# First stage of an encoder kernel: weights' products, x's transposes and the value groups in one written order

## The chip, the cores and the metric

The kernel runs on one core of a Trainium2 chip. The metric is the device time of one execution in microseconds, the median of several runs. The engines are TensorE (PE in the profile, its weight loads PEld), VectorE (DVE), ScalarE (ACT), GpSimd (POOL) and SyncE (SP, which here only issues DMAs).

## The reference

Two layers, each a token mixer and a convolutional MLP, on x of shape (1, 256, 1024) in float32. Only the beginning of the first layer matters here:

```python
def _rmsnorm(x, g):
    y = xf * lax.rsqrt(jnp.mean(xf * xf, axis=-1, keepdims=True) + EPS)
    return (y * g)

xn = _rmsnorm(h, norm1[layer])
u, q, k, v, g_pool, g_attn = jnp.split(xn @ w_in, SPLITS, axis=-1)
...   # pooling mixer on u, dilated attention on q, k, v, gates, output projection
h = h + ...
h = h + _conv_ffn(_rmsnorm(h, norm2[layer]), ...)
```

The values `v` are 1536 columns of `w_in`: three groups of 512.

## The kernel before

Every float32 product is made of three products of split numbers: a high part (`xuh`, `wh`) and a rest (`xul`, `wl`), with `hh`, `lh` and `hl` for high times high, rest of x times high weights, high x times rest of weights. ScalarE casts the high part, VectorE subtracts to get the rest. x's 256 tokens are two halves `t` of 128, its 1024 channels eight chunks `k` of 128.

The first layer starts with the values, since a row's norm can be applied to the finished sums. `begin_values_of_x` records, in an order written out by hand (`manual_schedule`), the first group of values: x comes in parts by SyncE's and ScalarE's DMA queues, TensorE transposes it (`turn_x`, `xt_ps`), ScalarE and VectorE split it (`keep`), and they split the weights chunk by chunk, scaled by the norm's gains (`split(k)`, `both(k)`: high part L255, rest L256; the gains are turned in `begin` and kept in `gcol`). `square` sums the squares of x's rows, GpSimd makes the root (`rs`), and `whole` adds `xuh` and `xul` into `xu` again, half of the channels at a time. The tiles of the weights in this group are named m (chunks 0 to 3), ybig (4, 5) and at (6, 7); from the second group on `wh` and `wl`, in pieces of two chunks.

`first_values` holds the second and the third group of values (L930), and scales `xu` by the root (`rows`, `r_ps`) and the gains into `x2`, which the products of queries, keys and pooling read (`by_tokens`, `t_ps`, L691). Before the change a scheduler places these instructions, and those of `load_params`, by its own costs. A group's four pieces are held until both halves of the tokens are done, one half after the other:

```python
for t in range(2):
    for n, (_, (wh, wl)) in enumerate(held):
        for j in range(2):
            ...
```

Weights come through a ring of three raw buffers of 1 MB (`W.load`, SyncE) and a ring of five split pieces. `W.get` splits some pieces ahead of use. A load waits until the raw buffer before it in the ring has been split. What follows the values (L1250 on) is written in its own order and is the same before and after.

Of the kernel before, what the change touches and what calls it, by code (L numbers as in the profile page):

```python
# [280 lines left out]
def encoder(ctx, tc, x, w_in, w_pool, pool_scale, w_a, w_b, w_o, norm1, norm2, w_up, conv_w,  # L281
# [85 lines left out]
    def begin():  # L367


        rows8 = sm.tile([KD, P], F32, tag="gain", bufs=1, name="grows")  # L370
        first, second = W.load_by(4), W.load_by(2)

        def part_of_x(queue, t, cc):
            queue.dma_start(out=h[:, t, cc], in_=xv[:, t, cc])

        nc.scalar.dma_start(out=rows8, in_=norm1[0].rearrange("(k p) -> k p", p=P))
        for t, queue in enumerate((nc.sync, nc.scalar)):
            part_of_x(queue, t, slice(0, 256))
# [12 lines left out]
        nc.vector.memset(mhalf, -0.5)  # L391
        ps = mmp.tile([P, P], F32, tag="mm", name="gain_ps")
        warm(ps, ones, WARM[0])
        nc.tensor.transpose(ps[:, 0:KD], rows8, ident[:KD, :KD])
        nc.vector.tensor_copy(gcol, ps[:, 0:KD])
        ps = mmp.tile([P, P], F32, tag="mm", name="warm_ps")
        warm(ps, ones, WARM[1])
        return lambda widths: warm(ps, ones, widths)
# [10 lines left out]
    def load_params():  # L409

        nc.sync.dma_start(out=edge.rearrange("p a b -> p (a b)"), in_=edges[0].partition_broadcast(P))
        for l in range(DEPTH):
# [3 lines left out]
            nc.sync.dma_start(out=rowst[88:96, :], in_=pool_scale[l].rearrange("(f p) -> f p", p=P))  # L416
            pt = mmp.tile([P, 512], F32, tag="mm", name="prm_ps")
            nc.tensor.transpose(pt[:, :96], rowst, ident[:96, :96])
            nc.vector.tensor_copy(prm[:, l, :], pt[:, :96])
            nc.vector.tensor_scalar_mul(hps[:, l, :], prm[:, l, 88:96], 0.5)  # L420

    bt = const.tile([P, HPG, NT * P], F32, name="bt")

# [343 lines left out]
    def begin_values_of_x():  # L767


        more = begin()  # L770
        W.gains = gcol

        raw_x = [
# [26 lines left out]
        def square(t, n):  # L800
            cc = HALVES[n]
            junk = sm.tile([P, 512], F32, tag="p", bufs=3, name="junk")
            if n == 0:
                nc.scalar.activation(
                    junk, h[:, t, cc], AF.Square, scale=D**-0.5, accum_out=ss[t][:, n : n + 1]
                )
            else:
                nc.vector.scalar_tensor_tensor(
                    out=junk, in0=h[:, t, cc], scalar=1.0 / D, in1=h[:, t, cc],
                    op0=ALU.mult, op1=ALU.mult, accum_out=ss[t][:, n : n + 1],  # L810
                )
            if n == 0:
                nc.gpsimd.tensor_scalar_add(ss[t][:, 3:4], ss[t][:, 0:1], EPS)
            else:
                nc.gpsimd.tensor_add(out=ss[t][:, 3:4], in0=ss[t][:, 3:4], in1=ss[t][:, 1:2])
                return nc.gpsimd.tensor_tensor(out=rs[t], in0=ss[t][:, 3:4], in1=mhalf, op=ALU.pow)

        def whole(n, tag):

            ks = slice(4 * n, 4 * n + 4)  # L820
            f = big.tile([P, 4, 2, P], F32, tag=tag, name="xu")
            nc.vector.tensor_add(out=f, in0=xuh[:, ks].bitcast(F32), in1=xul[:, ks].bitcast(F32))
            return f

        ps = [v_tile() for _ in range(2)]
# [27 lines left out]
        every = ("hh", "lh", "hl")  # L853
        keep = [turn_x((t,), 0, 2) for t in range(2)]
        more(WARM[2])
# [9 lines left out]
        products((0, 0, ("hl",)), (1, 0, ("hl",)))  # L865
        both(2)
        products((0, 1, ("hh", "lh")), (1, 1, ("hh", "lh")), (0, 1, ("hl",)), (1, 1, ("hl",)))
        both(3)
        square(0, 0)
        square(1, 0)  # L870
        square(0, 1)
        pool = square(1, 1)
        products((0, 2, ("hh", "lh")), (1, 2, ("hh", "lh")))
        keep = turn_x((0,), 4, 4)
        products((0, 2, ("hl",)), (1, 2, ("hl",)))
        keep()
        products((0, 3, every))
        keep = turn_x((1,), 4, 4)
        both(4)
        keep()  # L880
        W.load(5)
        products((1, 3, every), (0, 4, every))
        both(5)
        products((1, 4, every), (0, 5, every))
        f0 = whole(0, "q0")
        both(6)
        products((1, 5, every), (0, 6, every))
        both(7)
        products((1, 6, every), (0, 7, every))
        f1 = whole(1, "k0")  # L890
        pe = products((1, KD - 1, ("hh", "hl", "lh")))
# [6 lines left out]
        return rs, raw_x, (f0, f1), ps, pe  # L898

    def first_values(rs, raw_x, fs, done, pe, keep_values):  # L900
# [5 lines left out]
        with tc.issue_after(pe.ins):  # L906
            for t in range(2):
                nc.tensor.transpose(rows[:, t, :], rs[t][:, 0:1].to_broadcast([P, P]), ident)
        for k in range(0, KD, 2):
            f = fs[k // 4][:, k % 4 : k % 4 + 2]  # L910
            for j in range(2):
                nc.vector.scalar_tensor_tensor(
                    out=f[:, j], in0=f[:, j], scalar=gcol[:, k + j : k + j + 1], in1=rows,
                    op0=ALU.mult, op1=ALU.mult,
                )
            oh, ol = (x2[:, k : k + 2, part] for part in (0, 1))
            nc.scalar.copy(out=oh, in_=f)
            nc.vector.tensor_sub(out=ol, in0=f, in1=oh.bitcast(F32))
        ps = done
        for g in range(NG):  # L920
            held = [W.get() for _ in range(4)] if g + 1 < NG else []
            for t in range(2):
                keep_values(t, g, ps[t], rs)
            ps = [v_tile() for _ in range(2)]
            for t in range(2):
                for n, (_, (wh, wl)) in enumerate(held):
                    for j in range(2):
                        k = 2 * n + j
                        for m, (a, w) in enumerate(((xuh, wh), (xuh, wl), (xul, wh))):
                            nc.tensor.matmul(  # L930
                                ps[t], a[:, k, t, :], w[:, j, :], start=(k + m == 0),
                                stop=(k == KD - 1 and m == 2),
                            )
            for i, _ in held:
                W.free(i)
        return x2

    for l in range(DEPTH):
# [21 lines left out]
        if l == 0:  # L960
            with tc.manual_schedule():
                begun = begin_values_of_x()
            x2 = first_values(*begun, keep_values)
        else:
            for g in range(NG):
                held = begun[0] if g == 0 else [W.get() for _ in range(4)]
# [9 lines left out]
                    W.free(i)  # L976

        if l == 0:
            load_params()
# [515 lines left out]
```

## Time and profile before

| | |
|---|---|
| median of three runs | 855.9 us (854.67 to 855.96) |
| profiled execution | 854.77 us; span of its instructions 853.0 us |
| busy in the span | TensorE 844.8, its weight loads 705.7, VectorE 620.6, ScalarE 490.5, GpSimd 33.6 us |
| granted clock of TensorE | 0.998 |
| values, from the first product to the first t_ps | 5.73 to 41.15 us |

The page's busy times are for the whole program; the stage of the change is the first 5% of it. A row of the timeline has the start, the duration, engine, line, operation, output and inputs, shapes, how many such instructions follow one another, and in brackets the idle time before them with what ended it. TensorE's rows overlap, since its matmuls are pipelined: the distance from start to start is what one costs.

### The profile page before, as it was taken

What the parts mean: (1) busy time and instruction counts of PE and PEld (TensorE: products, weight loads), DVE (VectorE), ACT (ScalarE), POOL (GpSimd) and SP (SyncE); (2) the same over time, 40 slices, a digit from 0 to 9 for tenths busy, and PEclk for the clock granted to TensorE, in tenths of its full rate; (3) what the DMA queues carried; (4) which work ended last, traced back from release to release, by engine and by line L of the source; (5) the groups of instructions that cost most, each with busy time, mean ns of one, the idle gap of its engine ahead of it and who ended that gap; (6) DMA issues with size and microseconds to landing.
All of it is one profiled execution on the core that took longest, in us unless ns stands there. A gap on an engine that the chain in (4) does not pass through costs nothing.

```text
span 853.0 us, 11006 instructions
## 1 busy us (share of the span) xinstructions
PE 844.8 (99%) x3925; PEld 705.7 (83%) x3925; DVE 620.6 (73%) x885; ACT 490.5 (58%) x723; POOL 33.6 (4%) x96
## 2 busy tenths in 40 slices
PE   9999999999999999999999999999999999999997
PEld 7888888888888888888888888888888888888885
DVE  7958777757765976878655687868567767777774
ACT  7744566654543865657545454577454556556663
POOL 1700000000010000000000000000000100000000
PEclk9999999999999999999999999999999999999999
DMA  9699997895657879986726899868777489799941
GB/s 326 212 302 285 294 292 233 252 293 210 222 209 263 300 250 301 293 284 233 245 100 216 261 280 330 245 226 264 242 257 269 147 289 315 230 288 288 296 145 50
DMA packets 147678, 214.03 MB, mean 251 GB/s; under 512 B 7768, under 2 KB 68640, under 8 KB 147624
## 3 DMA queue, kind: packets, MB, share of 16 engines
q1 hardware_dynamic: 147320, 212.93, 76.8%
q8 instruction: 31, 0.51, 0.2%
q10 hardware_dynamic: 304, 0.40, 0.1%
q14 instruction: 23, 0.19, 0.1%
HBM read 186.02 MB, written 27.28 MB: 250 GB/s over the span
## 4 chain that ended last, share of the span: by engine, by line
PE 98%; DMA 1%; SPq 0%; DVE 0%; ACT 0%; issue 0%; DVEq 0%; ACTq 0%
PE t_ps L691 64%; PE v_ps L691 6%; PE res_ps L610 6%; PE res_ps L608 6%; PE res_ps L609 6%; PE v_ps L930 3%; PE pool_ps L595 1%; PE v_ps L839 1%; PE o_ps L1200 1%; PE s_ps L1152 1%; PE s_ps L1147 1%; PE o_ps L1196 1%; PE xt_ps L522 1%; DMA h<-in_x_dram 1%; PE xt_ps L787 0%; SPq L184 0%
## 5 line engine op out<-in xcount | busy, mean ns | idle before, releaser
L245 DVE TENSOR_TENSOR wl<-raw,wh 128x1024 fp32r<-128x1024 f32 x274 | 332.0, 1221 | 159.0 <-ACT wh L243 158.1
L691 PE MATMUL t_ps<-wh,x 128*128 128x512 f32 x1408 | 438.8, 390 | 0.0
L243 ACT CAST wh<-raw 128x1024 fp32r<-128x1024 f32 x274 | 286.3, 1052 | 211.5 <-PE t_ps L691 146.4
L691 PEld LDWEIGHTS t_ps<-wh,x 128*128 128x128 f32 x1408 | 264.3, 188 | 54.8
L691 PE MATMUL t_ps<-wl,x 128*128 128x512 f32 x704 | 273.9, 389 | 0.0
L691 PEld LDWEIGHTS t_ps<-wl,x 128*128 128x128 f32 x704 | 132.2, 188 | 27.3
L610 PE MATMUL res_ps<-wh,actk 128*128 128x512 f32 (+1 forms) x184 | 70.0, 380 | 0.0
L609 PE MATMUL res_ps<-wl,actq 128*128 128x512 f32 (+1 forms) x184 | 69.9, 380 | 0.0
L608 PE MATMUL res_ps<-wh,actq 128*128 128x512 f32 (+1 forms) x184 | 69.8, 380 | 0.0
L691 PE MATMUL t_ps<-wh,po 128*128 128x512 f32 x128 | 41.4, 395 | 0.0
L608 PEld LDWEIGHTS res_ps<-wh,actq 128*128 128x128 f32 x184 | 34.6, 188 | 6.6
L609 PEld LDWEIGHTS res_ps<-wl,actq 128*128 128x128 f32 x184 | 34.6, 188 | 6.6
L610 PEld LDWEIGHTS res_ps<-wh,actk 128*128 128x128 f32 x184 | 34.6, 188 | 6.6
L487 POOL TENSOR_SCALAR ss<-ss 128x1 f32<-128x1 f32 x8 | 2.2, 279 | 773.5 <-ACT junk L480 773.5
L691 PEld LDWEIGHTS t_ps<-wh,po 128*128 128x128 f32 x128 | 24.0, 188 | 4.9
L1373 ACT ACTIVATE y<-a,prm 128x256 f32<-128x256 f32 x44 | 26.5, 602 | 1.5
L608 PE MATMUL res_ps<-wh,m 128*128 128x512 f32 (+1 forms) x72 | 26.5, 368 | 0.0
L609 PE MATMUL res_ps<-wl,m 128*128 128x512 f32 (+1 forms) x72 | 26.3, 365 | 0.0
L741 DVE STREAM_TRANSPOSE crossing<-t_ps 128x512 f32<-128x512 f32 x40 | 26.2, 693 | 0.0
L610 PE MATMUL res_ps<-wh,m 128*128 128x512 f32 (+1 forms) x72 | 26.0, 366 | 0.0
L691 PE MATMUL v_ps<-wh,x 128*128 128x512 f32 x80 | 25.6, 392 | 0.0
L691 PE MATMUL t_ps<-wl,po 128*128 128x512 f32 x64 | 24.9, 390 | 0.0
(193 smaller groups left out, 931.1 us busy)
## 6 DMA issues: line engine op xcount, KB each, us to landing
raw<-in_w_in_dram SPq DMA_DIRECT2D x58, 1024.0 KB, 6.8
raw<-in_w_up_dram SPq DMA_DIRECT2D x40, 1024.0 KB, 7.1
raw<-in_w_down_dram SPq DMA_DIRECT2D x22, 1024.0 KB, 6.0
crossing<-crossing SPq DMA_DIRECT2D x22, 512.0 KB, 8.5
crossing<-way SPq DMA_DIRECT2D x16, 512.0 KB, 4.8
raw<-in_w_a_dram SPq DMA_DIRECT2D x8, 1024.0 KB, 5.1
raw<-in_w_o_dram SPq DMA_DIRECT2D x8, 1024.0 KB, 7.0
zga<-crossing SPq DMA_DIRECT2D x40, 128.0 KB, 3.7
```

The costliest lines, as they stand in the source:

```text
L243: inst = nc.scalar.copy(out=h, in_=src)
L245: inst = self.rests[i] = nc.vector.tensor_sub(out=l, in0=src, in1=h.bitcast(F32))
L522: nc.tensor.transpose(pt[:, k, :], xn[:, c0 : c0 + P], ident)
L595: nc.tensor.matmul(out, w(k), x, start=(steps is first and k == 0), stop=(steps is last and k == nk - 1), skip_group_check=turns["rest"],)
L608: nc.tensor.matmul(ps, ah, wh, start=first, stop=False, skip_group_check=on)
L609: nc.tensor.matmul(ps, ah, wl, start=False, stop=False, skip_group_check=on)
L610: nc.tensor.matmul(ps, al, wh, start=False, stop=last, skip_group_check=on)
L691: nc.tensor.matmul(ps, x2[:, 2 * n + j, part, t, :], w[:, j, :], start=(n + m == 0), stop=(n == last and m == 5),)
L741: nc.vector.transpose(out=y[:, t].rearrange("p q c j -> p c q j"), in_=rows[t])
L839: return nc.tensor.matmul(ps[t], a[:, k, t, :], w[:, k % 2, :], start=first, stop=last)
L930: nc.tensor.matmul(ps[t], a[:, k, t, :], w[:, j, :], start=(k + m == 0), stop=(k == KD - 1 and m == 2),)
L1373: nc.scalar.activation(y, a, AF.Identity, bias=b, scale=w1)
```

## The change

- `begin`: half of x's first part goes ahead of the gains on ScalarE's queue; seven warming matmuls and one more of full width in place of six and two of half width; the gains are turned between the two transposes of x.
- `begin_values_of_x`: another order, below. Both halves of the squares go to ScalarE. `whole` goes to GpSimd, both calls after the squares. The high part of chunk 2 goes to VectorE.
- `load_params` issues its DMAs behind the fifth weight load, and its transposes come one after each value group.
- `first_values`: written order. Each piece serves both halves of the tokens and is then freed; the scaling of `xu` is spread between the pieces.

```diff
-WARM = ((P,) * 6, (P // 2,), (P // 2,))
+WARM = ((P,) * 7, (P,))
-        nc.scalar.dma_start(out=rows8, in_=norm1[0].rearrange("(k p) -> k p", p=P))
         for t, queue in enumerate((nc.sync, nc.scalar)):
             part_of_x(queue, t, slice(0, 256))
+        nc.scalar.dma_start(out=rows8, in_=norm1[0].rearrange("(k p) -> k p", p=P))
...
-            nc.vector.tensor_add(out=f, in0=xuh[:, ks].bitcast(F32), in1=xul[:, ks].bitcast(F32))
+            nc.gpsimd.tensor_add(out=f, in0=xuh[:, ks].bitcast(F32), in1=xul[:, ks].bitcast(F32))
...
+        def one_by_one(*steps):
+            products(*((t, k, (kind,)) for k, kind in steps for t in range(2)))
...
-        products((0, 0, ("hh",)), (1, 0, ("hh",)), (0, 0, ("lh",)), (1, 0, ("lh",)))
+        one_by_one((0, "hh"), (0, "lh"))
+        both(1)
+        one_by_one((1, "hh"), (1, "lh"))
         keep = turn_x((0, 1), 2, 2)
-        both(1)
+        _, lo, hi = split(2)
+        hi()
         keep()
...
+        one_by_one((0, "hl"), (1, "hl"))
         both(3)
+        one_by_one((2, "hh"), (3, "hh"), (2, "lh"))
+        keep = [turn_x((0,), 4, 4)]
+        one_by_one((3, "lh"))
+        keep.append(turn_x((1,), 4, 4))
+        both(4)
+        W.load(5)
+        turn_params = load_params()
+        for k in keep:
+            k()
+        one_by_one((2, "hl"), (3, "hl"))
+        both(5)
+        one_by_one((4, "hh"), (4, "lh"), (4, "hl"))
         square(0, 0)
         square(1, 0)
+        both(6)
+        one_by_one((5, "hh"), (5, "lh"), (5, "hl"))
+        both(7)
         square(0, 1)
         pool = square(1, 1)
...
+        fs = [whole(n, tag) for n, tag in enumerate(("q0", "k0"))]
+        one_by_one((6, "hh"), (6, "lh"), (6, "hl"))
+        products((0, 7, every))
+        products((1, KD - 1, ("hh", "hl", "lh")))
...
+        for g in range(NG - 1):
             ps = [v_tile() for _ in range(2)]
+            for n in range(4):
+                at = 4 * g + n
+                for begun in scales[max(0, at - 1) : at]:
+                    next(begun)
+                i, (wh, wl) = W.get()
+                for begun in scales[max(0, at - 2) : at]:
+                    next(begun)
+                for j in range(2):
+                    k = 2 * n + j
+                    for m, (a, w) in enumerate(((xuh, wh), (xuh, wl), (xul, wh))):
+                        for t in range(2):
                             nc.tensor.matmul(
...
                 W.free(i)
+                if n == 0:
+                    for t in range(2):
+                        if g == 0:
+                            nc.tensor.transpose(
+                                rows[:, t, :], rs[t][:, 0:1].to_broadcast([P, P]), ident
+                            )
+                    for t in range(2):
+                        keep_values(t, g, done[t], rs)
+            if g < DEPTH:
+                turn_params(g)
+            done = ps
```

TensorE's queue at the beginning, from the first products on (xt_ps are the transposes of x), before:

```order
L839 MATMUL v_ps<-m_138,xuh 128x512 x2
L839 MATMUL v_ps<-m_138,xul 128x512 x2
L787 MATMUL xt_ps<-ident,h 128x128 x4
L839 MATMUL v_ps<-m_138,xuh 128x512 x3
L839 MATMUL v_ps<-m_138,xul 128x512
```

and after:

```order
L841 MATMUL v_ps<-m_138,xuh 128x512 x2
L841 MATMUL v_ps<-m_138,xul 128x512 x2
L841 MATMUL v_ps<-m_138,xuh 128x512 x2
L841 MATMUL v_ps<-m_138,xul 128x512 x2
L795 MATMUL xt_ps<-ident,h 128x128 x4
L841 MATMUL v_ps<-m_138,xuh 128x512 x8
L841 MATMUL v_ps<-m_138,xul 128x512 x2
L795 MATMUL xt_ps<-ident,h 128x128 x4
```

Four products of chunk 1 now stand ahead of the second transposes, and ten products instead of twelve between those and the third.

ScalarE's queue from chunk 1 to the second group's first weights (ybig and at are the weights of chunks 4 to 7, junk the squares), before:

```order
L255 ACTIVATE m_138<-raw_92,gcol 128x512
L793 CAST xuh<-xt_ps 128x512
L255 ACTIVATE m_138<-raw_92,gcol 128x512 x2
L804 ACTIVATE junk,ss<-h 128x512 x2
L793 CAST xuh<-xt_ps 128x4x128
L255 ACTIVATE ybig_205<-raw_100,gcol 128x512
L793 CAST xuh<-xt_ps 128x4x128
L255 ACTIVATE ybig_205<-raw_100,gcol 128x512
L255 ACTIVATE at_228<-raw_100,gcol 128x512 x2
L255 ACTIVATE wh_252<-raw_103,gcol 128x512 x2
```

and after:

```order
L255 ACTIVATE m_138<-raw_92,gcol 128x512
L801 CAST xuh<-xt_ps 128x512
L255 ACTIVATE m_138<-raw_92,gcol 128x512
L255 ACTIVATE ybig_188<-raw_100,gcol 128x512
L801 CAST xuh<-xt_ps 128x4x128 x2
L255 ACTIVATE ybig_188<-raw_100,gcol 128x512
L811 ACTIVATE junk,ss<-h 128x512 x2
L255 ACTIVATE at_224<-raw_100,gcol 128x512 x2
L811 ACTIVATE junk,ss<-h 128x512 x2
L255 ACTIVATE wh_261<-raw_103,gcol 128x512 x2
```

The first ybig (chunk 4) now stands ahead of both casts of x's second half, and four squares ahead of the second group's weights.

GpSimd's queue from the squares on, after (before, L440 followed the last power at once):

```order
L815 TENSOR_SCALAR ss<-ss 128x1 x2
L817 TENSOR_TENSOR ss<-ss 128x1
L818 TENSOR_TENSOR rstd<-ss,mhalf 128x1
L817 TENSOR_TENSOR ss<-ss 128x1
L818 TENSOR_TENSOR rstd<-ss,mhalf 128x1
L824 TENSOR_TENSOR xu<-xuh,xul 128x1024 x2
L448 COPY fsb<-rbt 4x1 x4
```

Both sums of x stand behind the powers and ahead of the small copies of the bias table. On VectorE, where they stood between the weights' rests, nothing takes their place.

More of the change, by code (lines that the diff above doesn't have):

```diff
@@ L391, in begin, with gains @@
         nc.vector.memset(mhalf, -0.5)
-        ps = mmp.tile([P, P], F32, tag="mm", name="gain_ps")
+        ps = mmp.tile([P, P], F32, tag="mm", name="warm_ps")
         warm(ps, ones, WARM[0])
[L394 to L398, printed above, removed]
+        def gains():
+            gp = mmp.tile([P, P], F32, tag="mm", name="gain_ps")
+            nc.tensor.transpose(gp[:, 0:KD], rows8, ident[:KD, :KD])
+            nc.vector.tensor_copy(gcol, gp[:, 0:KD])
+        return gains, lambda widths: warm(ps, ones, widths)
     def warm(ps, a, widths):
@@ L411, in load_params @@
         nc.sync.dma_start(out=edge.rearrange("p a b -> p (a b)"), in_=edges[0].partition_broadcast(P))
+        rows = []
         for l in range(DEPTH):
@@ L416, in load_params, with turn @@
             nc.sync.dma_start(out=rowst[88:96, :], in_=pool_scale[l].rearrange("(f p) -> f p", p=P))
+            rows.append(rowst)
+        def turn(l):
             pt = mmp.tile([P, 512], F32, tag="mm", name="prm_ps")
-            nc.tensor.transpose(pt[:, :96], rowst, ident[:96, :96])
+            nc.tensor.transpose(pt[:, :96], rows[l], ident[:96, :96])
             nc.vector.tensor_copy(prm[:, l, :], pt[:, :96])
             nc.vector.tensor_scalar_mul(hps[:, l, :], prm[:, l, 88:96], 0.5)
+        return turn
     bt = const.tile([P, HPG, NT * P], F32, name="bt")
@@ L767, in begin_values_of_x @@
     def begin_values_of_x():
-        more = begin()
+        gains, more = begin()
         W.gains = gcol
@@ L802, in square @@
             junk = sm.tile([P, 512], F32, tag="p", bufs=3, name="junk")
[L803 to L811, printed above, removed]
+            nc.scalar.activation(
+                junk, h[:, t, cc], AF.Square, scale=D**-0.5, accum_out=ss[t][:, n : n + 1]
+            )
             if n == 0:
@@ L851, in products @@
             return last
+        def one_by_one(*steps):
+            products(*((t, k, (kind,)) for k, kind in steps for t in range(2)))
         every = ("hh", "lh", "hl")
-        keep = [turn_x((t,), 0, 2) for t in range(2)]
-        more(WARM[2])
+        keep = [turn_x((0,), 0, 2)]
+        gains()
+        keep.append(turn_x((1,), 0, 2))
+        more(WARM[1])
         _, lo, hi = split(0)
@@ L860, in begin_values_of_x @@
         lo()
-        products((0, 0, ("hh",)), (1, 0, ("hh",)), (0, 0, ("lh",)), (1, 0, ("lh",)))
+        one_by_one((0, "hh"), (0, "lh"))
+        both(1)
+        one_by_one((1, "hh"), (1, "lh"))
         keep = turn_x((0, 1), 2, 2)
-        both(1)
+        _, lo, hi = split(2)
+        hi()
         keep()
-        products((0, 0, ("hl",)), (1, 0, ("hl",)))
-        both(2)
-        products((0, 1, ("hh", "lh")), (1, 1, ("hh", "lh")), (0, 1, ("hl",)), (1, 1, ("hl",)))
+        lo()
+        one_by_one((0, "hl"), (1, "hl"))
         both(3)
+        one_by_one((2, "hh"), (3, "hh"), (2, "lh"))
[10 more added lines that the diff above has]
+        one_by_one((4, "hh"), (4, "lh"), (4, "hl"))
         square(0, 0)
         square(1, 0)
+        both(6)
+        one_by_one((5, "hh"), (5, "lh"), (5, "hl"))
+        both(7)
         square(0, 1)
         pool = square(1, 1)
[L873 to L891, printed above, removed]
+        fs = [whole(n, tag) for n, tag in enumerate(("q0", "k0"))]
+        one_by_one((6, "hh"), (6, "lh"), (6, "hl"))
+        products((0, 7, every))
+        products((1, KD - 1, ("hh", "hl", "lh")))
         W.load(6)
@@ L897, in begin_values_of_x, with first_values @@
         W.queue_behind((act, dve, pool), 4)
-        return rs, raw_x, (f0, f1), ps, pe
-    def first_values(rs, raw_x, fs, done, pe, keep_values):
+        return rs, raw_x, fs, turn_params, ps
+    def first_values(rs, raw_x, fs, turn_params, done, keep_values):
         xuh, xul = raw_x
@@ L905, in first_values, with scale @@
         rows = mmp.tile([P, 2, P], F32, tag="mm", name="r_ps")
[L906 to L909, printed above, removed]
+        def scale(k):
             f = fs[k // 4][:, k % 4 : k % 4 + 2]
@@ L915, in first_values @@
                 )
+            yield
             oh, ol = (x2[:, k : k + 2, part] for part in (0, 1))
             nc.scalar.copy(out=oh, in_=f)
+            yield
             nc.vector.tensor_sub(out=ol, in0=f, in1=oh.bitcast(F32))
[L919 to L923, printed above, removed]
-            ps = [v_tile() for _ in range(2)]
[L925 to L929, printed above, removed]
+            yield
+        scales = [scale(k) for k in range(0, KD, 2)]
+        for g in range(NG - 1):
+            ps = [v_tile() for _ in range(2)]
+            for n in range(4):
[9 more added lines that the diff above has]
+                        for t in range(2):
                             nc.tensor.matmul(
@@ L933, in first_values @@
                             )
-            for i, _ in held:
                 W.free(i)
+                if n == 0:
[3 more added lines that the diff above has]
+                                rows[:, t, :], rs[t][:, 0:1].to_broadcast([P, P]), ident
+                            )
+                    for t in range(2):
[3 more added lines that the diff above has]
+            done = ps
+        for t in range(2):
+            keep_values(t, NG - 1, done[t], rs)
         return x2
@@ L978, in encoder @@
         if l == 0:
-            load_params()
             with tc.issue_after(W.behind[1].ins):
```

4 lines of the change are left out of this document (3 added, 1 removed).

## The prediction

> **What bounds the kernel now.** I read the page first, then the chain of waits of the first 45 us, then the busy time by stretches, then TensorE's own waits.
>
> ```profile
> PE 844.8 (99%) x3925; PEld 705.7 (83%) x3925; DVE 620.6 (73%) x885; ACT 490.5 (58%) x723; POOL 33.6 (4%) x96
> PE xt_ps L787 <- DMA h<-in_x_dram: 1.2, 2, 0.8
> 0.00:5.73 5.73, 4.16 (x22) 3.69 (x22) 0.86 (x4) 1.70 (x3) 0.69 (x6) 1.00 0.64 168
> 5.73:7.43 1.70, 1.35 (x6) 0.67 (x5) 1.52 (x4) 1.05 (x2) 0.00 (x0) 1.00 0.92 307
> 7.43:19.31 11.88, 11.88 (x60) 9.66 (x60) 10.79 (x18) 10.65 (x20) 2.74 (x6) 1.00 1.05 400
> 19.31:41.15 21.84, 21.84 (x101) 18.07 (x98) 20.80 (x37) 15.47 (x23) 15.51 (x50) 1.00 0.63 212
> ```
>
> In the stretches, the columns are length, then PE, PEld, DVE, ACT and POOL busy, granted clock, DMA share and GB/s. TensorE never rests after 7.43 us. The whole program is one stream of matmuls, so a change is worth what it adds to this stream or takes out of its gaps. The order of instructions changes only in the first 44 us; the rest can only shift. In that stretch VectorE is nearly as full as TensorE, and ScalarE fills 10.65 of 11.88 us in the first part: they have little to lend.
>
> ```profile
> 5.73 0.89 PE L839 MATMUL v_ps<-m,xuh 128*128 128x512 f32 x2
> 7.43 0.63 PE L787 MATMUL xt_ps<-ident,h 128*128 128x128 f32 x4 [0.35 <-DMA h<-in_x_dram]
> 12.88 3.97 PE v_ps L839 x17
> 19.17 0.38 PE L908 MATMUL r_ps<-ident,rstd 128*128 128x128 f32 x2
> 19.55 11.58 PE v_ps L930 x51
> 41.15 0.39 PE L691 MATMUL t_ps<-wh,x 128*128 128x512 f32 x1
> ```
>
> (The third and fifth rows are from the chain, the others from the timeline; start, length.) The first product starts at 5.73, the query/pool stage at 41.15: 35.42 us. A product costs 11.58/51 = 0.227 us (0.233 in the first group, 3.97/17). 144 products take 32.7 us, twelve transposes of x inside the stretch about 1.1 (three fours, 0.38 from 7.43 to the product at 7.81), the others 0.25: 34.0. Only 1.4 us can be recovered here by order alone, 0.17% of the time. What a measurement of this kernel can tell from no change is about 0.2%, 1.7 us.
>
> **The change part by part.** *The start.* The first product needs the first quarter of the first weights, scaled by VectorE:
>
> ```profile
> 5.10 0.48 DVE L261 TENSOR_SCALAR m<-raw,gcol 128x512 fp32r<-128x512 f32 x1 [1.08 <-DMA raw<-in_w_in_dram]
> 3.85 0.17 DVE L395 COPY gcol<-gain_ps 128x8 f32<-128x8 f32 x1 [3.00 <-PE gain_ps L394]
> 6.13 0.72 ACT L255 ACTIVATE m<-raw,gcol 128x512 fp32r<-128x512 f32 x1
> ```
>
> SyncE's queue ahead of it is unchanged, so 5.10 stays. The gains now stand behind half of x's first part on ScalarE's queue, but their copy at 3.85 has 1.25 us to give; cost 0, at worst some 0.2. The seventh warming matmul lies in time in which TensorE waits for x: 0. I leave the first product at 5.73.
>
> *Second chunk ahead of the next transposes.* Four products of chunk 1 now fill the 0.35 us wait before 7.43. Their high part starts on ScalarE at 6.13, as before (it stood right behind another cast there, so its data was no later), and is there at 6.85: products 6.9 to 7.8, then transposes to 8.2. At 8.2 TensorE has done eight products and the four transposes; before, it had that at 7.81 + 4 x 0.233 + a first step of 0.1, 8.8. So 0.6 us is gained here.
>
> *The fifth chunk.* The new order puts chunk 4's high part on ScalarE ahead of both casts of x's second half (both(4) stands before keep). Chunks 4 and 5 come with the second transfer's first half. When does it land?
>
> ```profile
> 6.12 0.77 SPq L165 DMA_DIRECT2D raw<-in_w_in_dram  x1
> DMA to landing us min/median/max: 9.1/9.1/9.1
> 11.31 0.59 ACT L793 CAST xuh<-xt_ps 128x512 fp32r<-128x512 f32 x1 [0.18 <-PE xt_ps L787]
> 11.80 0.72 ACT L255 ACTIVATE ybig<-raw,gcol 128x512 fp32r<-128x512 f32 x1
> 9.81 0.62 ACT L804 ACTIVATE junk<-h 128x512 f32<-128x512 f32 x1
> 15.25 5.10 ACT L255 ACTIVATE wh<-raw,gcol 128x512 fp32r<-128x512 f32 x8
> 13.53 0.69 DVE L794 TENSOR_TENSOR xul<-xt_ps,xuh 128x512 fp32r<-128x512 f32 x1 [0.23 <-ACT xuh L793]
> 14.15 0.75 DVE L256 SCALAR_TENSOR_TENSOR ybig<-raw,gcol,ybig 128x512 fp32r<-128x512 f32 x1
> ```
>
> The next-but-one transfer (the first two rows) lands at 6.12 + 9.1 = 15.2; 1.5 MB lie between, 3.9 us at 400 GB/s, which gives 11.3 (bound above: 11.8, where ScalarE used it without a DMA wait; below: 2.6 MB lie up to its end, 168 x 5.73 + 307 x 1.70 = 1.5 MB are moved by 7.43, the rest takes 2.8 us at 400 GB/s: 10.3). So ScalarE, free at 9.7 (the cast of x's second quarter from 8.5, then chunk 3's high part), waits until 11.4, and both casts stand behind it: chunk 4's high part to 12.0, casts start 12.0 and 12.5 (0.49 apart by 11.31 to 11.80). VectorE's rest of the chunk and the two rests of x (0.75, 0.69, 0.69) end at 14.1; TensorE, which could have had them from about 13, waits 0.6 to 0.9 us. Chunk 4 is done at 14.9, 18 products more at 19.05. Before, this point is 19.17 less the one product drawn ahead of it, 18.94. The front is therefore worth **+0.1 us**, between -0.5 (landing 10.3, TensorE itself the limit) and +0.6 (landing 11.8): the gain of the second chunk is given back by the fifth.
>
> Chunk 2's high part moves to VectorE (0.48 by the row at 5.10), which has nothing else before x's rest comes at 9.1: 0.
>
> *Squares to ScalarE.* Two more, 0.62 each; ScalarE now runs chunk 5, two squares, chunks 6 and 7, two squares, and starts the next group's weights at 17.4 instead of 15.25 (0.63 apart: 5.10 less one, over 7). It still stays ahead of TensorE's 19.05 by one half piece at 18.1; hidden, but the lead shrinks. This matters for the next step.
>
> *x's sums to GpSimd.* VectorE loses two of 1.22 us. GpSimd gets two adds that read two SBUF operands of 128x1024, behind its adds and powers of the norm. The last square ends at 17.6; an add and a power after it (0.61 and 0.56, below, the add less when alone) end at 18.5 to 18.8.
>
> ```profile
> 14.82 1.22 DVE L822 TENSOR_TENSOR xu<-xuh,xul 128x1024 f32<-128x1024 f32 x1
> 427.28 0.19 POOL L489 TENSOR_TENSOR ss<-ss 128x1 f32<-128x1 f32 x1 [1.40 <-ACT junk L480]
> 428.94 1.20 POOL L489 TENSOR_TENSOR ss<-ss 128x1 f32<-128x1 f32 x1 [1.47 <-ACT junk L480]
> 428.88 1.21 DVE L245 TENSOR_TENSOR wl<-raw,wh 128x1024 fp32r<-128x1024 f32 x1
> L815 POOL TENSOR_TENSOR ss<-ss 128x1 f32<-128x1 f32 x2 | 1.2, 614 | 0.1
> L816 POOL TENSOR_TENSOR rstd<-ss,mhalf 128x1 f32<-128x1 f32 x2 | 1.1, 561 | 0.2
> masks.py:199 POOL TENSOR_SCALAR_AFFINE_SELECT ident<-ident 128x128 f32<-128x128 f32 x1 | 0.3, 293 | 0.1
> L440 POOL COPY fsb<-rbt 4x1 f32<-4x1 f32 (+12 forms) x57 | 18.6, 381 | 11.7 <-DMA fsb<-in_onehot_dram 11.7
> ```
>
> The same tiny add takes 0.19 us alone, and 1.20 when VectorE's two-operand subtraction starts just ahead: it ends 0.05 after that one. So the two engines exclude each other there, and GpSimd gets in between two VectorE instructions. The trace has no long GpSimd instruction, so it does not show VectorE held in turn. The Trainium skill (SBUF — State Buffer, "SBUF: two separate sides") calls the pair of ports an exclusive lock for the whole instruction, whoever starts first, if VectorE reads two SBUF operands and GpSimd reads SBUF. By that rule the sums hold VectorE; by the rows alone they might only wait themselves, and this step would cost 0. I forecast that they hold it, since an exclusion that works one way and lets both in at once the other way would be strange.
>
> Price of one sum: as low as VectorE's 1.22; as high as eight times the one row of this engine over 128x128, 8 x 0.293 = 2.34. I take 2.34, the nearest row by engine and width. The Trainium skill (GPSIMD Engine Reference, "3.1 Elementwise") has 4497 ns for 2048 elements; an estimate of half is 2.25, and the sum below would be 0.2 lower.
>
> VectorE's order: the first half piece of the next group's rests runs at 18.15 to 18.9; the first sum holds until 21.25; second half piece 22.0; the second sum until 24.35; third half piece 25.1. TensorE wants this third one at 19.05 + 12 x 0.227 + 0.14 (transposes of the root) + 2 x 0.227 = 22.35. It stands for 25.15 - 22.35 = **2.8 us**, in two waits (second and third half piece). In general twice the price less 1.9: 0.5 at 1.22. Afterwards VectorE gains 0.6 us on TensorE with each half piece (0.75 against 1.36), so nothing more is added.
>
> *Pieces serve both halves, scaling between pieces.* The same 96 products; r_ps and prm move, and count the same. The scaled x waits for both sums, 21.25 and 24.35, before VectorE reaches them at about 27 and 32: hidden. The fifth weight load stands behind six small parameter loads and a landing; it issues near 20.6 instead of 17.39:
>
> ```profile
> 17.39 0.40 SPq L165 DMA_DIRECT2D raw<-in_w_in_dram  x1
> raw<-in_w_in_dram SPq DMA_DIRECT2D x58, 1024.0 KB, 6.8
> ```
>
> With 6.8 us it is there at 27.4, when ScalarE reaches it; TensorE needs it after 35. 0.
>
> Sum: +0.1 + 2.8 = +2.9 against the profiled execution, 854.77 (span 853.0 and 1.77 around it): 857.7. The median of the runs, 855.9, is 1.1 above the profiled one, whose time is like the lowest run's; on it the sum gives 858.8. I take the middle, 858.2.
>
> **The rivals.** *Not slower: the sums never hold VectorE* (GpSimd waits for gaps, as the 57 copies did: they took 18.6 us among VectorE's work). Place: the second half piece at about 20.9. It decides if VectorE's next rest still ends before 20.8. Then only the front counts, +0.1 (-0.5 to +0.6): 854.9, on the median 856.0. For it: in the trace VectorE's durations beside the copies are its usual ones. Against it: those copies are of four partitions and a few elements.
>
> *Faster: the second transfer lands near 10.3 and the sums hide.* Then all gaps close: at most -1.4, 853.4, on the median 854.5; beyond 0.2% only if the first product comes earlier too.
>
> *Slower still: the two-operand add costs double the one-operand row, 4.7 us each.* Twice that less 1.9 is 7.5: 862.4.
>
> **How the numbers follow.** Sums hold VectorE: 0.66, of which 0.60 is over 0.2% (prices above about 1.8 us) and 0.06 within. No hold: 0.22, of which 0.21 within and 0.01 faster. All gaps close: 0.09, of which 0.05 faster, 0.04 within. Double price: 0.03, slower. Faster 0.06, same 0.31, slower 0.63. The likeliest case's own range is 855.8 to 860.1 (prices 1.4 to 3, that is 0.9 to 4.1 us, with the front's 0.1, on either base). The range starts at 854.9, into the case without a hold, and ends at 860.3; it leaves out the fast case, the lower part of the second and the double price.
>
> **What would show it.** Right: ScalarE idle from 9.6 to about 11.4 before the fifth chunk; VectorE idle twice by about 2.3 us near 19 to 24.5 while GpSimd runs L824; TensorE waiting there on wl, twice, 2.8 us in all; first t_ps at about 44. Wrong: the sums lasting 3 us or more while VectorE's rests go on at 0.67 us apart beside them, or first t_ps at 41.5 or earlier. The front is wrong if TensorE does not wait between 12.5 and 14.5.

## The result and the profile after

| | before | after |
|---|---|---|
| median | 855.16 us (854.44 to 855.96, 6 runs) | 857.95 us (857.54 to 858.85, 6 runs) |
| profiled execution, span | 854.77, 853.0 us | 858.85, 857.0 us |
| first product of the second group of values | 18.94 us (19.17, where the first group ends, less the one product drawn ahead) | 20.46 us |
| first t_ps | 41.15 us | 45.07 us |

The changed kernel is slower by 2.8 us, a ratio of 1.0033 [1.002, 1.0046]. 858.2 was forecast.

First the page of after, and its busy time in the two stretches that were shown of before (length, PE, PEld, DVE, ACT, POOL, granted clock, DMA share, GB/s):

```profile
PE 848.1 (99%) x3925; PEld 707.6 (83%) x3925; DVE 622.1 (73%) x880; ACT 490.7 (57%) x726; POOL 36.8 (4%) x98
```

```profile
7.43:19.31 11.88, 11.88 (x53) 9.25 (x52) 6.97 (x11) 7.52 (x17) 1.03 (x4) 1.00 1.03 374
19.31:41.15 21.84, 20.01 (x88) 15.84 (x87) 21.39 (x31) 13.96 (x23) 18.27 (x50) 1.00 0.57 168
```

The page shows next to nothing. In the second stretch TensorE runs 20.01 of 21.84 us, where it ran all of it before. VectorE looks as busy as it was (21.39 against 20.80) with fewer instructions, 31 against 37, and that is the trace of the cause: some of them became long. The waits of TensorE up to 50 us (in total, times, longest) name the tile:

```profile
PE v_ps L944 <- DVE wl L256: 1.8, 2, 0.9
PE warm_ps L405 <- PEq L1504: 0.8, 1, 0.8
```

The timeline of after around these two waits, GpSimd, VectorE, TensorE:

```profile
20.22 2.53 POOL L824 TENSOR_TENSOR xu<-xuh,xul 128x1024 f32<-128x1024 f32 x1
22.70 2.84 POOL L824 TENSOR_TENSOR xu<-xuh,xul 128x1024 f32<-128x1024 f32 x1
19.73 3.56 DVE L256 SCALAR_TENSOR_TENSOR wl<-raw,gcol,wh 128x512 fp32r<-128x512 f32 x2 [1.04 <-ACT wh L255]
23.22 2.87 DVE L256 SCALAR_TENSOR_TENSOR wl<-raw,gcol,wh 128x512 fp32r<-128x512 f32 x1
23.35 0.73 PE L944 MATMUL v_ps<-wl,xuh 128*128 128x512 f32 x2 [0.91 <-DVE wl L256]
26.15 0.73 PE L944 MATMUL v_ps<-wl,xuh 128*128 128x512 f32 x2 [0.91 <-DVE wl L256]
```

And the durations of this rest of the weights (min, median, max in ns), from the answer on the tile wl:

```profile
L256 DVE SCALAR_TENSOR_TENSOR wl<-raw,gcol,wh x10: 739/744/2896, 19.7 to 30.0; 128x512 fp32r<-128x512 f32 x10
```

Before, the same answer was:

```profile
L256 DVE SCALAR_TENSOR_TENSOR wl<-raw,gcol,wh x16: 742/745/748, 18.4 to 35.4; 128x512 fp32r<-128x512 f32 x16
```

A rest takes 0.74 us. Two of them now take 2.90 and 2.87: each begins while a sum runs on GpSimd, and ends about 0.55 us behind it. The second sum is shut out in turn: it is listed from 22.70, but with 2.84 us, 0.3 longer than the first, which fits a start at 23.30, where the first held rest ends. So the held time is inside VectorE's own instruction; as idle time of VectorE it does not appear at all.

The other part of the loss lies ahead of it, in the first group. Timeline of after, ScalarE and TensorE:

```profile
12.70 0.72 ACT L255 ACTIVATE ybig<-raw,gcol 128x512 fp32r<-128x512 f32 x1 [1.16 <-DMA raw<-in_w_in_dram]
20.46 0.61 PE L944 MATMUL v_ps<-wh,xuh 128*128 128x512 f32 x2
45.07 0.48 PE L699 MATMUL t_ps<-wh,x 128*128 128x512 f32 x1
```

Chunk 4 of the weights lands at 12.70, and the second group begins at 20.46 instead of 18.94: 1.52. From there to the first t_ps it is 24.61 us, against 41.15 - 18.94 = 22.21 before: 2.40. Together 3.92, which is the whole shift of t_ps, and nearly all of the 4.08 between these two executions. This execution is the slowest of the changed kernel's first six, by 0.9 over their median; the front part differs from one execution to the next, as the experiments show.

### The profile page after: what moved, and what is told of

Same layout as the page of the kernel before. It is cut to its first block, busy times and chain, and to the rows that moved or that the text cites. A ratio compares the mean times of both kernels' runs of the same rounds, so it can differ in the third digit from the quotient of the medians.

```text
span 857.0 us, 11009 instructions
## 1 busy us (share of the span) xinstructions
PE 848.1 (99%) x3925; PEld 707.6 (83%) x3925; DVE 622.1 (73%) x880; ACT 490.7 (57%) x726; POOL 36.8 (4%) x98
## 4 chain that ended last, share of the span: by engine, by line
PE 98%; ACT 1%; DVE 1%; issue 0%; DVEq 0%; ACTq 0%
PE t_ps L699 64%; PE v_ps L699 6%; PE res_ps L617 6%; PE res_ps L616 6%; PE res_ps L618 6%; PE v_ps L944 2%; PE pool_ps L603 1%; PE o_ps L1227 1%; PE s_ps L1179 1%; PE v_ps L841 1%; PE s_ps L1174 1%; PE o_ps L1223 1%; PE xt_ps L530 1%; DVE wl L256 1%; PE warm_ps L405 0%; PE xt_ps L795 0%
```

## The experiments

Two quantities are read from each profile beside the time: where the second group's first product starts (the front), and how long it is from there to the first t_ps (the stall; 22.2 us without one). A piece of weights is two chunks; a half piece is one chunk, six products and one rest of 128x512, and TensorE spends 6 x 0.227 = 1.36 us on it.

The kernels were run in three series, each with its own runs of the kernel before: 855.15 us (27 runs) beside both sums on VectorE, sums in gaps, only the sums moved and sums in eight; 855.53 (17) beside the two kernels with the casts first, the changed kernel once more and each sum twice; 855.06 (21) beside sums in four and one sum in a gap. The kernel before itself differs by 0.47 us between series, so smaller differences across series show nothing. A ratio is against the kernel before of the same series.

What the two quantities add reaches the end: in all ten profiles of the changed order, the span less the start of the first t_ps is 811.9 to 812.0 us, and 811.85 before.

**Both sums back on VectorE, at the same place.**

```diff
-            nc.gpsimd.tensor_add(out=f, in0=xuh[:, ks]..., in1=xul[:, ks]...)
+            nc.vector.tensor_add(out=f, in0=xuh[:, ks]..., in1=xul[:, ks]...)
```

> The changed kernel with both sums of x on VectorE, at the same place of the written order (behind the rests of chunk 7). Theory (the sums on GpSimd hold VectorE's next two rests, which cost TensorE 2.4 us in the profile after): the two long rests of 2.9 us go, VectorE has 2 x 1.22 us of its own ahead of the second group's rests instead, for which it has about 1 us of idle time and 0.4 us of lead, so some 0.2 to 1 us comes back: 1.4 to 2.2 us faster than the changed kernel, 855.8 to 856.5. Rival (the front, whose first eight products ran at 0.427 us each, is the whole loss): no change, 857.9.

856.25 us (855.63 to 856.9, 11 runs), ratio 1.0012 [1.0003, 1.0021]. Timeline, VectorE; then TensorE's wait on wl:

```profile
17.52 2.35 DVE L824 TENSOR_TENSOR xu<-xuh,xul 128x1024 f32<-128x1024 f32 x2
```

```profile
PE v_ps L944 <- DVE wl L256: 0.3, 1, 0.3
```

The engine alone is worth 1.7 us of the 2.8. The sums' own 2.35 us still delay VectorE's rests a little: 42.49 - 19.67 = 22.82 from the second group to t_ps.

**The sums on VectorE, in its gaps:** the edit above, and the first sum moved behind chunk 5's rest; the second stays behind chunk 7's.

```diff
         both(5)
+        fs = [whole(0, "q0")]
...
-        fs = [whole(n, tag) for n, tag in enumerate(("q0", "k0"))]
+        fs.append(whole(1, "k0"))
```

> The changed kernel with both sums on VectorE, the first behind the rest of chunk 5, the second behind that of chunk 7, where VectorE stood idle for 1.1 and 1.0 us in the profile after. Theory: the whole 2.4 us come back, 855.4 to 855.8, and what is left over the kernel before is the front alone. Rival (the front is the loss): 857.9.

855.51 us (855.24 to 856.43, 11 runs), ratio 1.0004 [0.9995, 1.0013]. Nothing waits on wl any more; 41.38 - 19.19 = 22.19. So the sums cost the changed kernel 857.95 - 855.51 = 2.4 us, and all the rest of the change no more than can be measured (855.51 against 855.15).

**The kernel before, with its two sums on GpSimd and nothing else changed.**

```diff
-            nc.vector.tensor_add(out=f, in0=xuh[:, ks]..., in1=xul[:, ks]...)
+            nc.gpsimd.tensor_add(out=f, in0=xuh[:, ks]..., in1=xul[:, ks]...)
```

> The kernel before with nothing changed but the engine of the two sums: GpSimd instead of VectorE. They start behind the powers at about 14.0 us and hold VectorE's rests of chunks 5 and 6. Theory: two rests take 2.9 us instead of 0.75, VectorE saves 2.4 us of its own, and TensorE waits for the rest of chunk 6 at about 17: 2.5 to 3.3 us slower than the kernel before, about 858. Rival (no hold that matters, VectorE is relieved): 0 to 0.5 us faster.

858.52 us (857.74 to 859.29, 5 runs), ratio 1.0037 [1.0024, 1.0049]. Timeline, GpSimd and VectorE, then TensorE's waits:

```profile
12.85 5.37 POOL L822 TENSOR_TENSOR xu<-xuh,xul 128x1024 f32<-128x1024 f32 x2
13.69 2.29 DVE L256 SCALAR_TENSOR_TENSOR ybig<-raw,gcol,ybig 128x512 fp32r<-128x512 f32 x1
15.90 3.54 DVE L256 SCALAR_TENSOR_TENSOR at<-raw,gcol,at 128x512 fp32r<-128x512 f32 x2
```

```profile
PE v_ps L839 <- DVE at L256: 1.1, 1, 1.1
PE v_ps L839 <- DVE ybig L256: 1.0, 1, 1.0
```

This one edit makes the kernel before slower by 3.4 us, a little more than expected and more than the whole change does (2.8). At another place, with other rests (ybig and at), two sums hold two rests. In its profile the first t_ps starts 2.2 us later than before (43.36 against 41.15), and 0.7 more is lost behind it; that part was not followed up.

**The sums in eight adds of 128x256, and in four of 128x512,** still on GpSimd and at the changed kernel's place. The work and its engine stay; the length of one instruction changes.

```diff
-            nc.gpsimd.tensor_add(out=f, in0=xuh[:, ks]..., in1=xul[:, ks]...)
+            for j in range(4):
+                nc.gpsimd.tensor_add(out=f[:, j], in0=xuh[:, 4 * n + j]..., in1=xul[:, 4 * n + j]...)
```

> The changed kernel with each sum on GpSimd in four adds of 128x256 instead of one of 128x1024. Theory (one hold lasts one GpSimd instruction, and the engines take turns): each of eight rests takes about 0.7 us longer instead of two that take 2.1 longer; a rest and its add together, about 1.4 us, go at TensorE's pace of 1.36 us for half a piece, so TensorE waits 0 to 0.6 us instead of 2.4: 855.5 to 856.3. Rival (what counts is the sum of GpSimd's time on the ports, in whatever portions): no change, 857.9 or a little more.

> The changed kernel with its two GpSimd sums cut into four adds of 128x512 each... half as long a hold as in the changed kernel, twice as many. New theory (a held rest costs what its distance to the rest before exceeds TensorE's 1.36 us by): a sum of 128x512 takes about 1.2 to 1.4, so four rests follow each other by 1.4 to 1.7; 0 to 0.3 each, together 0 to 1.2 less a distance of 0.4 to 0.8: 855.5 to 856.2. Rival (the held time counts in full, however it is cut): the changed kernel's 857.5 to 858.3.

In eight: 855.59 us (854.85 to 856.59, 11 runs), ratio 1.0002 [0.9993, 1.0011], stretch 42.23 - 20.04 = 22.19. In four: 856.42 (855.91 to 856.94, 11 runs), ratio 1.0015 [1.0006, 1.0024], stretch 42.33 - 19.57 = 22.76; a little more than expected. First of the kernel with eight, then of that with four, the timeline's row of GpSimd and the durations of wl's rests:

```profile
19.50 8.89 POOL L825 TENSOR_TENSOR xu<-xuh,xul 128x256 f32<-128x256 f32 x8
```

```profile
L256 DVE SCALAR_TENSOR_TENSOR wl<-raw,gcol,wh x13: 739/1224/1229, 19.0 to 33.7; 128x512 fp32r<-128x512 f32 x13
```

```profile
19.02 6.52 POOL L826 TENSOR_TENSOR xu<-xuh,xul 128x512 f32<-128x512 f32 x4
```

```profile
L256 DVE SCALAR_TENSOR_TENSOR wl<-raw,gcol,wh x13: 739/741/1787, 18.5 to 33.5; 128x512 fp32r<-128x512 f32 x13
```

The two engines take turns, one instruction each. In eight pieces the sums take longer in all (8.89 us), and most rests are still held, to 1.22 us. But one add and one rest follow each other every 8.89/8 = 1.11 us on average, and TensorE needs a half piece only every 1.36: the hold costs nothing. In four they follow every 6.52/4 = 1.63 us on average, which is too late. How much that costs is worked out below, for all kernels together.

**Chunk 4's high part behind the two casts of x,** as in the kernel before, once in the changed kernel and once together with the sums in gaps.

```diff
+        for k in keep:
+            k()
         both(4)
         W.load(5)
         turn_params = load_params()
-        for k in keep:
-            k()
```

> The changed kernel with one edit: the two casts of chunks 4 to 7 of x stand ahead of chunk 4's high part on ScalarE's queue, so that they no longer wait behind its landing. Theory (the fifth chunk's term: the casts' wait costs TensorE about half a microsecond behind the first product of chunk 4): in the kernel with the sums in gaps TensorE spent 1.67 us on the four products of chunk 4 from 12.96 that take 0.91 without a wait, 0.76 lost; with the casts first the high part ends about 13.2 and some 0.25 is lost, so 0.3 to 0.6 us come back, if nothing behind takes them: 857.3 to 857.7. Rival (the front's loss lies elsewhere, or the held rests, which are late by the GpSimd sums' own time, take the gain back): the changed kernel's time, 857.8 to 858.1.

> Both mends together: the sums on VectorE in its gaps (first behind chunk 5's rest, second behind chunk 7's), and the two casts ahead of chunk 4's high part. Nothing is held here, so what the front gains should reach the end. Theory: 855.5 less 0.3 to 0.6, which is 854.8 to 855.2, level with the kernel before (855.15) or just under it. Rival (the casts' wait is hidden): 855.4 to 855.6.

Alone: 857.81 us (857.5 to 857.98, 6 runs), ratio 1.0029 [1.0018, 1.0041]: the gain is not there. With the sums in gaps: 855.25 (854.99 to 857.23, 11 runs), ratio 1.0001 [0.9993, 1.001]: between the two expectations, and 0.26 below 855.51, in another series, which cannot be told from nothing. In the profiles the second group begins at 19.00 and at 19.03, earlier than in any of the eight profiles of the other order; ScalarE, which comes to chunk 4 at 12.65 and 12.68, finds it there, so when it landed is not seen. From these the term can be read directly. Chunk 4's row on ScalarE with the sums in gaps, and with one sum held (below), each with the second group's first product:

```profile
11.53 0.72 ACT L255 ACTIVATE ybig<-raw,gcol 128x512 fp32r<-128x512 f32 x1 [1.92 <-DMA raw<-in_w_in_dram]
19.19 0.62 PE L945 MATMUL v_ps<-wh,xuh 128*128 128x512 f32 x2
```

```profile
12.73 0.72 ACT L255 ACTIVATE ybig<-raw,gcol 128x512 fp32r<-128x512 f32 x1 [3.32 <-DMA raw<-in_w_in_dram]
20.40 0.61 PE L945 MATMUL v_ps<-wh,xuh 128*128 128x512 f32 x2
```

| landing of chunk 4 | 11.51 | 11.53 | 11.91 | 12.01 | 12.18 | 12.38 | 12.70 | 12.73 |
|---|---|---|---|---|---|---|---|---|
| second group begins | 19.16 | 19.19 | 19.57 | 19.67 | 19.84 | 20.04 | 20.46 | 20.40 |

Seven of the eight stand 7.65 to 7.67 apart and the eighth (the changed kernel's first profile) 7.76: in this order the front is the landing plus 7.66 us, and the landing differs by 1.2 us between executions. In the changed kernel an earlier front does not reach the end in full, since the sums then hold the rests all the same: with the casts first the stretch behind it was 43.64 - 19.00 = 24.64, against 44.13 - 19.84 = 24.29 in the changed kernel's second profile, so that 0.49 of 0.84 us were left at the first t_ps. By the medians, casts first are worth 857.97 - 857.81 = 0.16 in the changed kernel and 0.26 with the sums in gaps, neither clear of the noise.

**The changed kernel once more,** with nothing edited.

> The changed kernel once more, for a second profile and a paired time. In its first profile the first eight products ran at 0.43 us each, and the second group began at 20.46; in four of the other profiles these products ran at 0.23. Theory (the moment of full rate differs from one execution to the next and the kernel doesn't set it): the same median of 857.5 to 858.3, and a profile that may open earlier, with the second group's first product between 18.9 and 20.5. Rival (the change of order itself brings the slow opening): first products at 0.43 us again and the second group at 20.4 or later. In both, two rests of about 2.9 us beside the two sums.

857.97 us (857.12 to 858.41, 6 runs), ratio 1.003 [1.0018, 1.0042]. Its profile has the first products at 0.23 us each, the second group at 19.84, the first t_ps at 44.13, and the same two waits:

```profile
PE v_ps L944 <- DVE wl L256: 1.5, 2, 0.9
```

So the change doesn't bring the slow products of the first profile each time; it does bring the held rests.

**Each sum computed twice:** four GpSimd instructions instead of two.

```diff
-            nc.gpsimd.tensor_add(out=f, in0=xuh[:, ks]..., in1=xul[:, ks]...)
+            for _ in range(2):
+                nc.gpsimd.tensor_add(out=f, in0=xuh[:, ks]..., in1=xul[:, ks]...)
```

> The changed kernel with the suspected cost doubled: each of the two GpSimd sums is computed twice into the same tile, four instructions of 128x1024 instead of two. Theory (each GpSimd sum holds exactly one VectorE rest for its whole length, about 2.15 us beyond the 0.74 that a rest takes, and VectorE's lead of 1.9 us is spent once): four rests held, 4 x 2.15 - 1.9 = 6.7 us over the kernel with the sums in gaps, which is about 862.2, range 860.8 to 863.2; four rests of 2.9 us stand in the trace. Rival 1 (what costs is the late rest at the hand-over between the engines, once): about the changed kernel's 858. Rival 2 (what costs is that the sums end late, for the scaling that reads them): less than 858.5, with no wait on wl beyond the two.

860.79 us (860.16 to 862.52, 5 runs), ratio 1.0069 [1.0055, 1.0084]: 2.8 over the changed kernel, less than forecast. Timeline of GpSimd; then TensorE's wait on wl:

```profile
18.62 10.92 POOL L825 TENSOR_TENSOR xu<-xuh,xul 128x1024 f32<-128x1024 f32 x4
```

```profile
PE v_ps L945 <- DVE wl L256: 3.8, 4, 1.1
```

Four rests held, four waits, as expected; both rivals fall. The size did not fit: 46.33 - 19.16 = 27.17, a stall of 4.98 instead of 6.7. The expectation charged a hold with what it adds to a rest, 2.15. But a rest need not be done every 0.74 us; TensorE asks for one every 1.36. Its products with a held rest start 2.80 us apart (24.56 and 27.36), so a hold costs 2.80 - 1.36 = 1.44, and what VectorE was ahead of TensorE comes off once.

**One sum in a gap, one on GpSimd.**

```diff
-            nc.gpsimd.tensor_add(out=f, ...)        # both calls after chunk 7
+            (nc.vector, nc.gpsimd)[n].tensor_add(out=f, ...)   # first call after chunk 5
```

> The first sum on VectorE behind chunk 5's rest, only the second on GpSimd. New theory, from the traces so far: from its first product of a half piece to the next TensorE takes 1.36 us, a held rest follows the one before by 2.8; so each held rest costs 1.44, less TensorE's distance to VectorE (0.4 to 0.8), which is spent once. One hold: 0.6 to 1.0 us over the kernel with the sums in gaps, one wait on wl, 856.1 to 856.6. The prediction's formula (n times the price less 1.9, price 2.34): 0.4, about 855.9. Rival (half of what two holds cost): 1.2, 856.7.

855.97 us (855.21 to 856.45, 11 runs), ratio 1.0007 [0.9999, 1.0016]. Half the cost of two (856.7) is out: no run reached it. Between the prediction's formula (855.9) and the new theory (856.1 and up) the time doesn't decide, and it cannot be told from that of the kernel with both sums in gaps either (1.0004 [0.9995, 1.0013]). The expected wait on wl is not there. GpSimd's row and the durations of wl's rests:

```profile
20.49 2.55 POOL L824 TENSOR_TENSOR xu<-xuh,xul 128x1024 f32<-128x1024 f32 x1
L256 DVE SCALAR_TENSOR_TENSOR wl<-raw,gcol,wh x14: 736/739/2901, 19.4 to 33.0; 128x512 fp32r<-128x512 f32 x14
```

A rest was held to 2.90 us and TensorE did not wait for it: 42.63 - 20.40 = 22.23. But it is not the rest that the first sum of the changed kernel holds. This sum begins 1.13 us behind VectorE's first rest (20.49 against 19.36), that one 0.49 (20.22 against 19.73), in large part because GpSimd's last power took 1.02 us here instead of 0.55. So two rests are done when the sum gets its turn, and the third is held. One hold was free for a VectorE that was two rests ahead; what one hold of the second rest would cost was not measured.

**One sum for all of them,** worked out after the runs. The last held rest ends 0.55 us behind the last GpSimd sum, as read in the profile after. TensorE, if nothing held it up, would ask for it 1.36 us times n after its first product with a rest of the second group, where n counts the half pieces between. By as much as the first moment is behind the second, TensorE should stall; the last column has what each profile shows, its stretch less the 22.19 of the kernel with the sums in gaps. In us:

| | last sum ends | first product with a rest | n | worked out | stall |
|---|---|---|---|---|---|
| changed kernel, first profile | 25.54 | 20.91 | 2 | 2.46 | 2.42 |
| changed kernel, second profile | 24.61 | 20.29 | 2 | 2.15 | 2.10 |
| casts first | 24.12 | 19.45 | 2 | 2.50 | 2.45 |
| each sum twice | 29.54 | 19.62 | 4 | 5.03 | 4.98 |
| sums in four | 25.54 | 20.02 | 4 | 0.63 | 0.57 |
| sums in eight | 28.39 | 20.49 | 8 | below 0 | 0.00 |
| one sum in a gap | 23.04 | 20.86 | 2 | 0.01 | 0.04 |

The stalls come out to 0.06 us. Nothing but the held rests is needed to account for them.

## Why the prediction was right, step by step

- *The sums hold VectorE:* right, and shown from five sides: by the two long rests, by the engine alone (856.25, 855.51), by the edit alone (858.52), by cutting the instruction (855.59), and by doubling it (860.79). The rival rested on 57 copies beside which VectorE's durations stayed usual; whether these left VectorE alone for being short, for their four partitions or for reading one operand was not tried. The Trainium skill (SBUF — State Buffer, "SBUF: two separate sides") calls the shared ports an exclusive lock for the whole instruction; these traces agree, with rests of 2.90 and 2.87 us beside sums of 128x1024, and 1.22 beside 128x256.
- *The price of a sum, 2.34:* close. The first sum takes 2.53 from 20.22, of which 0.26 pass until the running rest ends at 20.48: 2.27. Part of this is luck: the row that was scaled is of another operation, with one operand.
- *The stall, 2.8:* the right mechanism and places (second and third half piece), the size somewhat high: 2.10 to 2.45 in three profiles, 2.4 by the medians. The prediction let a whole rest of 0.75 follow each sum, a period of 3.09; the held rest ends 0.55 behind the sum and the period is 2.80. (Its own steps give 25.08 - 22.37 = 2.7 rather than 25.15 - 22.35, which changes nothing.)
- *How it would look:* wrong in form. "VectorE idle twice by about 2.3 us" is not in the trace; the held instruction itself is long. And the waits on wl add up to 1.8, less than the stall of 2.42: a wait is counted from the listed end of the two products before it, which is 0.62 behind their start where they cost 0.45, and the two products behind a wait take 0.73. ScalarE's idle time ahead of chunk 4 was there, and TensorE's wait near 13 in the second profile (0.54 us ahead of 13.43); in the first, TensorE's slow opening fills it.
- *The fifth chunk:* the chain behind the landing was right to 0.1 us (11.4 to 19.05 forecast, 7.65; measured 7.66), the landing was not: 11.51 to 12.73 instead of 11.3 with a bound of 11.8. That bound came from one execution of before, in which ScalarE found the chunk there at 11.80. The transfers were also slower than the forecast's 400 GB/s: from 6 to 11.5 us the DMAs moved 305 to 348 GB/s in the eight profiles of this order, 368 in the one of before. Why the landing moves so much is not shown. So the front gives 19.2 to 20.5 in place of 19.05, and the "+0.1" was too small for the executions profiled. The medians put it at 855.51 - 855.15 = +0.4, not distinguishable from 0.1.
- *The start:* the gains' copy came at 4.35 to 5.07 instead of 3.85, as late as was allowed for, and the first product at 5.91 in after and at 5.19 to 5.59 in the other nine profiles of the changed order, against 5.73. Little hangs on it, since the front follows chunk 4's landing.
- *The second chunk:* right, except in the first profile of after. Eight products and four transposes were forecast for 8.2 us; the next products begin at 8.12 with the sums in gaps and at 7.88 in the second profile of after, against 8.8 before.
- *Squares to ScalarE:* with the landing at 11.51, in the kernel with each sum twice, ScalarE begins the next group's weights at 17.38 (forecast 17.4) and VectorE its rests at 18.14 (18.15). With the sums in gaps nothing waits for it; the lead that it shortens is the one that the sums then use up.
- *Pieces, scaling, fifth load:* nothing to be seen, 0. The load issues at 21.78 in after (forecast 20.6).
- *The base:* 2.8 on 855.16 is 857.95; 2.9 was forecast, on a middle of 855.3. Front and stall were off by +0.3 and -0.4; that they cancel is luck.

## What to carry to other kernels

Work moved to an engine that is nearly idle is not free if the two engines shut each other out: look for long instructions there (here sums of 128x1024 with two operands), beside a VectorE that is on the path. The same work can cost 2.4 us or nothing, by the length of one instruction: if one of theirs and one of yours fit into the time in which the consumer uses one result (here 1.36 us), the exclusion costs nothing; otherwise each pair costs the difference, less what the held engine was ahead. And where a queue is written by hand, a step that waits for a transfer ties the steps behind it to the landing, even those whose data is there; here the landing moved by 1.2 us between executions. What the other order is worth here is below what the medians can tell (0.16 and 0.26).

No version was found that beats the kernel before: the changed order with the sums in gaps and the casts first is level with it, 855.25 against 855.53.

## What the runs showed of the hardware

An engine that is shut out shows as busy. In the stretch from 19.31 to 41.15 VectorE is busy for 98% of the time (21.39 of 21.84 us; 95% before) while it does less work; only the number of instructions and the largest duration gave it away.

TensorE's full rate at the start did not come at the same time in each execution, and the granted clock did not show it. In nine of the ten profiles of the changed order the products follow each other by 0.23 us from about 6 us on; in the tenth, the first of the changed kernel, by 0.43 until 9.46. TensorE's first products in the two profiles of the same changed kernel:

```profile
6.90 1.05 PE L841 MATMUL v_ps<-m,xul 128*128 128x512 f32 x2
7.75 1.05 PE L841 MATMUL v_ps<-m,xuh 128*128 128x512 f32 x2
```

```profile
6.14 0.63 PE L841 MATMUL v_ps<-m,xul 128*128 128x512 f32 x2
6.60 0.62 PE L841 MATMUL v_ps<-m,xuh 128*128 128x512 f32 x2
```

In the first, two products are 0.85 us apart (6.90 to 7.75), in the second 0.46; the clock's column of the stretch from 5.91 to 9.46 in the first reads 1.00. By the table of landings it cost about 0.1 us at the second group's start (7.76 against 7.66), since what followed waited for chunk 4 anyway. Whether something in the kernel could fix the moment was not tried.
